# Second norm with a tile for each half's root, half 1 first, and the later fold instructions queued behind half 0's root

## The chip, the core and the metric

The kernel runs on one core of one Trainium2 chip. The metric is the device time of one execution in microseconds (us). TensorE (PE) multiplies matrices, VectorE (DVE), ScalarE (ACT) and GpSimd (POOL) work elementwise, and SyncE (SP) issues most of the loads; each engine takes its instructions in the order of its own queue, and a DMA issued from an engine's queue stands in that queue too.

## What is computed

The reference is a two-layer backbone over 1024 tokens of 1024 channels, in float32:

```python
for l in range(2):
    shift, scale, gate = split(silu(c) @ mod_w[l] + mod_b[l], 3)
    h = modulate(rmsnorm(x, norm_g[l]), shift, scale)        # h * (1 + scale) + shift
    if l == 0:  out = even_mixer(h, ...)   # convolution branch A and RG-LRU branch B, one out-projection
    else:       out = odd_mixer(h, ...)    # the pooling mixer, below
    x = x + gate * out
return rmsnorm(x, final_g)

def odd_mixer(h):
    u, g = split(h @ w_in, [2048])
    d = multiscale_pool(u)                 # four groups of 512 channels, each with its own window
    y = einsum("bngi,gij->bngj", d, w_grp) * scale
    return (y * silu(g)) @ w_out
```

`rmsnorm(x)` is x * rsqrt(mean over channels of x^2 + 1e-6) * g. The change is in the norm of the second layer, and in the tile of its helper, which the norm of the first layer uses as well.

## The kernel before

**Tiles.** x is held transposed: eight tiles of 128 channels by 1024 tokens, each in two halves of 512 tokens. Float32 products are made from rounded parts: `split` (line 101) writes the rounded high part with a cast on ScalarE (L102) and the rest with a subtract on the engine named (L103), and a product takes three matmuls, high-high, low-high and high-low. The out-projection `woa` and the v, g and wo products use `quad`, a seven-product scheme over 2 x 2 blocks whose weights `wquad` (lines 950 on) prepares from two loaded tiles `wr_...`, with sums such as `ws_v0` (L969).

**The folds.** The pooling mixer's group matrix and its input projection are both constant, so their product is formed once per group: `fold(g, ...)` (lines 236 to 263), a generator. It first loads the two halves of the group matrix (`graw_g_0`, `graw_g_1`), casts them on ScalarE (`gh`, L102) and subtracts on VectorE (`gl`, L103). That is the work up to its first `yield`. Then it loads four weight tiles (`wr_wu_g_0..3`) with the high part cast on ScalarE (`wh_wu`) and the low part on GpSimd (`wl_wu`), up to the second `yield`. Then for each of the four, and two strips of it, it runs 12 matmuls into a PSUM tile (`fold_g_kp_s`, L256 to L258), copies that on ScalarE (`fo_g_kp_s`, L261) and stores it to DRAM with a DMA from ScalarE's queue (L262), a `yield` behind every second strip. Groups 2 and 3 are left for this place. The stored products are the v weights that `wquad` loads later.

**Shared buffers.** `graw`, `wr_wu` and the `wr_v` tiles all use the pool tag "wr" with two buffers, so two chains of reuse run through the place: graw_3_0, wr_wu_3_0, wr_wu_3_2, wr_v0_0 in the one and graw_3_1, wr_wu_3_1, wr_wu_3_3, wr_v0_1 in the other. A load waits until the subtract that read the buffer's previous content is done, on VectorE for graw and on GpSimd for wr_wu. The `fo` tiles use a pool of two buffers: a copy waits for the store of the copy before the last.

**The norm.** Every out-projection row that is finished adds its square to `n1acc0` or `n1acc1` (L1265 on ScalarE, L1266 on VectorE), one for each half. `rstd_cols` (lines 194 to 208) then makes the root: four matmuls sum each column into one PSUM column (L200), ScalarE takes the Sqrt (L201, with a table load ahead of it), VectorE the reciprocal (L202) and a diagonal matrix `dg_...` (L204), and one matmul of ones with the diagonal puts the root into all 128 partitions (L207). The `rc` tile between Sqrt and diagonal has tag "rc" and one buffer in `hpool` and in `spool`, the same for both halves. After that, `scaled` (L1325) multiplies each tile half by the root and its channel scale on VectorE, 16 instructions in all; `split_x` (L1320 on ScalarE, L1321 and L103 on VectorE) makes the rounded parts of the block sums (`x_b11`, `x_t1`, `x_t3`, ...), and the quads for v (`qa_v`, `qb_v`, `qc_v`) multiply them with the folded weights. The tile `rc_n1h` and its like read `rc_n` in the profile, where the numbers at a name's end are left out (so also `dg_n`, `ms_n`, `gh`, `gl`).

**The order.** A scheduler places the instructions on each engine at build time, from the order of the program, from priorities, and from the context `tc.issue_after(ins)`: what is written inside comes behind `ins` in the queue, if it is on the engine of `ins`. In the program the column sums and roots of both halves (L1293) stand after the last out-projection product, and behind them come two steps of fold 2 and two of fold 3 (graw and weights), then the rest of both folds; the v stage follows. `load` (lines 106 to 114) puts every load on SP's queue.

**The first norm** (line 464) uses `rstd_cols` in the same way, with `rc_x`, `dg_x` and `ms_x`, at about 34 to 41 us of the span.

Of the kernel before, what the change touches and what calls it, by code (L numbers as in the profile page):

```python
# [9 lines left out]
F32 = mybir.dt.float32  # L10
F32R = mybir.dt.float32r
AF = mybir.ActivationFunctionType
# [3 lines left out]
P = 128  # L16
# [5 lines left out]
H = 512  # L22
# [33 lines left out]
def body(ctx, tc, xT, ctxT, cc, ccol, modT, modW, win, gw, wout, wu, grp, wg, wo1, small, edge, ident, outT):  # L56
    nc = tc.nc
    mult, add, sub = ALU.mult, ALU.add, ALU.subtract
# [22 lines left out]
    def ttile(name):  # L81
        return tpool.tile([P, H], F32, tag="t", name=name)

    def atile(name):
        return apool.tile([P, NR * PW], F32, tag="acc", name=name)

    def psum(name):
        return pm.tile([P, H], F32, tag="mm", name=name)
# [6 lines left out]
    def banks(name, n):  # L95
        if n % 2:
            t = wide(name)
            return [t[:, h] for h in HALF]
        return [pc.tile([P, H], F32, tag=f"c{i}", name=f"{name}_{i}") for i in range(2)]
# [46 lines left out]
    def col(o, n=1):  # L146
        return sm[:, o : o + n]
# [3 lines left out]
    eps_r = base.tile([P, 1], F32, name="eps_r")  # L151
# [39 lines left out]
        nc.vector.reciprocal(acc, rt[:, :n])  # L191


    def rstd_cols(acc, name, idD, rpool, wn):
        n = acc.shape[-1]
        nt = n // P
        ps, root = banks(f"ms_{name}", wn)
        r = rpool.tile([P, H // P], F32, tag="rc", name=f"rc_{name}")[:, :nt]
        for c in range(nt):
            nc.tensor.matmul(ps[:, c : c + 1], acc[:, c * P : (c + 1) * P], ones[:, 0:1], start=True, stop=True)  # L200
        nc.scalar.activation(r, ps[:, :nt], AF.Sqrt, bias=eps_r)  # L201
        nc.vector.reciprocal(r, r)  # L202
        t = ttile(f"dg_{name}")[:, :n]
        nc.vector.tensor_tensor(out=t.rearrange("p (c t) -> p c t", t=P),  # L204
                                in0=idD.unsqueeze(1).to_broadcast([P, nt, P]),
                                in1=r.unsqueeze(2).to_broadcast([P, nt, P]), op=mult)
        nc.tensor.matmul(root[:, :n], ones, t, start=True, stop=True)  # L207
        return root[:, :n]

# [25 lines left out]
    def fold(g, raw_tile, out_tile, g_tile=None, w_tile=None):  # L235
        g_tile = g_tile or dtile
        gh, gl = [], []
        for i in range(2):
            raw = raw_tile(f"graw_{g}_{i}")
            load(raw, grp[g, i])  # L240
            th = g_tile(f"gh_{g}_{i}", F32R)
            tl = g_tile(f"gl_{g}_{i}", F32R)
            split(raw, th, tl, nc.vector)
            gh += [th[:, 0:H], th[:, H:D]]
            gl += [tl[:, 0:H], tl[:, H:D]]
        yield
        if w_tile is not None:
            ws = [wload(wu[g, kp], f"wu_{g}_{kp}", nc.gpsimd, out=w_tile[kp]) for kp in range(KT // 2)]
            yield
        for kp in range(KT // 2):  # L250
            wh, wl = wload(wu[g, kp], f"wu_{g}_{kp}", nc.gpsimd) if w_tile is None else ws[kp]
            for s in range(2):
                ps = psum(f"fold_{g}_{kp}_{s}")
                for i in range(4):
                    kc = slice(i * 2 * P + s * P, i * 2 * P + (s + 1) * P)
                    nc.tensor.matmul(ps, wh[:, kc], gh[i], start=(i == 0), stop=False)  # L256
                    nc.tensor.matmul(ps, wh[:, kc], gl[i], start=False, stop=False)
                    nc.tensor.matmul(ps, wl[:, kc], gh[i], start=False, stop=(i == 3))  # L258
                dst = wfold[g][:, :, 2 * kp : 2 * kp + 2, :]
                o = out_tile(f"fo_{g}_{kp}_{s}")  # L260
                nc.scalar.copy(o, ps)  # L261
                nc.scalar.dma_start(dst[:, :, s, :].rearrange("m p c -> p m c"),  # L262
                                    o.rearrange("p (m c) -> p m c", c=P))
            yield
# [33 lines left out]
    with ExitStack() as sctx:  # L298
# [28 lines left out]
        acc = [atile("ssq0"), atile("ssq1")]  # L327
# [91 lines left out]
        for i, t in enumerate((cL, cC)):  # L419
            ps = banks(f"c_{i}", i)  # L420
# [41 lines left out]
        load(idx, ident)  # L462
        modulation(2)
        rx = [rstd_cols(acc[h][:, :H], f"x{h}", idx, spool, h) for h in range(2)]
        mod_row(1)
        mod_row(0)
# [186 lines left out]
    with ExitStack() as actx:  # L653
# [88 lines left out]
        for j in range(KT):  # L742
# [20 lines left out]
            name = "gb0" if final else f"xb{j + 1}"  # L763
# [6 lines left out]
            if state is None:  # L770
                for m in range(2 * KT, 3 * KT):
# [5 lines left out]
                    in1=col(O_MB + 2 * KT, KT), op=add)  # L777
# [9 lines left out]
            for h in range(2):  # L787
                ps = psum(f"va{j}_{h}")
# [5 lines left out]
            name = "gb1" if final else f"vg{j + 1}"  # L794
# [95 lines left out]
    hpool = ctx.enter_context(tc.tile_pool(name="hpool", bufs=1))  # L890
# [330 lines left out]
    for i in range(KH):  # L1221
        for j in (i, KH + i) if i else ():
# [3 lines left out]
            for h in range(2):  # L1226
                ps = psum(f"ga{j}_{h}")
# [30 lines left out]
    nacc = [atile("n1acc0"), atile("n1acc1")]  # L1258
# [24 lines left out]
    idD = cH[:, :P]  # L1283
# [3 lines left out]
    fold2 = fold(2, wr_tile, vtile, d2tile, [None, None, dtile, dtile])  # L1287
    fold3 = fold(3, wr_tile, vtile, d2tile, [dtile] * 4)
    for m in range(0, KT, 2):
        w0 = woa(m, w0, (lambda: wo_weights(m + 2)) if m < KT - 2 else None)  # L1290
    dsh = hpool.tile([P, KH], F32, name="dsh")
    nc.vector.tensor_tensor(out=dsh, in0=m1[:, 0, KH:KT], in1=m1[:, 0, 0:KH], op=sub)
    rs = [rstd_cols(nacc[h][:, :H], f"n1{h}", idD, hpool, h) for h in range(2)]  # L1293
    for f in (fold2, fold2, fold3, fold3):
        next(f)
    for f in (fold2, fold3):
        for _ in f:
            pass

    def ring_x(name):  # L1300
        return xpool.tile([P, S], F32R, tag="x", name=name)
# [37 lines left out]
    for i in range(KH):  # L1339
# [3 lines left out]
        t = block_sums(b11, b12, b21, b22, ttile(f"xt3_{i}"), nc.vector)  # L1343
# [343 lines left out]
    def last_half0(m, w, ahead=None):  # L1687
        p1, p2, p3, p4, p5, p6, p7 = w
        a, d, b = psum(f"qa_l{m}"), psum(f"qd_l{m}"), psum(f"qb_l{m}")
        (x0, x1_), (y0, y1) = [[x1[m + i][:, h] for h in HALF] for i in range(2)]  # L1690
        prod(a, p1, ops["b11"], True, False)
        with tc.high_priority(offset=EVAC):
            evac = nc.scalar.copy(b, a)
        mm = prod(d, p4, ops["t4"], True, True)
        with tc.high_priority(offset=EVAC):
            gated(m + 1, y0, d)
        nxt = None
        if ahead is not None:
# [20 lines left out]
    wb, _, _ = last_half0(m, wa, ahead)  # L1719
# [157 lines left out]
```

## Time and profile before

| what | value |
|---|---|
| time, median of 3 runs | 1294.53 us (1294.15 to 1294.73) |
| the profiled execution's own time | 1297.47 us |
| its span, first to last instruction | 1295.7 us |
| granted TensorE clock, mean | 0.996 |
| ScalarE, share of the span busy | 49% |
| GpSimd, share of the span busy | 27% |
| second norm's column sums of half 1 begin (PE) | 769.57 us |
| first Sqrt of the second norm (ACT) | 784.29 us |
| last fold matmul (PE) | 813.96 us |

The profile is of one execution. A row of a timeline names the start in us, the duration, the engine and source line, the operation, the tile written and those read, the shape, and in square brackets the idle time of the engine ahead of it with what ended that wait. `SPq` and `ACTq` are DMA issues from SP's and ScalarE's queues. `x16` at a row's end is a run of instructions of one kind, and the duration then is from the first to the last. A row of waits names what waited, for what, the sum, the number and the longest. Idle time of an engine matters only where PE waits for what that engine does.

### The profile page before, as it was taken

The page shows a single profiled execution, that of the slowest core. Times are in us where ns is not written, and L with a number is a line of the kernel's source. Part 1 is how long each engine was busy: PE and PEld are TensorE (multiplying, and loading weights), DVE is VectorE, ACT ScalarE, POOL GpSimd, SP SyncE. Part 2 cuts the span into 40 slices and gives each one's busy share as a digit, 9 for nine tenths or more (in the row PEclk, how much of TensorE's full clock was granted, in tenths as well). Part 3 has the DMA queues.
Part 4 walks back from the last instruction along what each step waited for, and adds up shares of the span by engine and source line. Part 5 has one row for each costly group of instructions (what it writes and reads, how often), then busy time and mean ns, then how long its engine had stood idle before and what let it go on. Part 6 is the DMA issues. An engine that isn't in the chain of part 4 may idle for free.

```text
span 1295.7 us, 15787 instructions
## 1 busy us (share of the span) xinstructions
PE 1274.6 (98%) x5630; PEld 1025.1 (79%) x5630; DVE 1143.5 (88%) x1758; ACT 637.3 (49%) x936; POOL 354.7 (27%) x180
## 2 busy tenths in 40 slices
PE   9999999999999999999999999999999999999997
PEld 4468888888888888888887887788888888778786
DVE  6979999999999989998789758998989987877876
ACT  4343666566657633237335346744334444644543
POOL 3063655575657613543210022000000000000002
PEclk9999999999999999999999999999999999999998
DMA  9934111121112133532555356244233324868723
GB/s 365 359 117 151 58 41 66 41 74 42 65 41 90 66 106 119 179 141 85 169 194 200 111 191 192 75 153 155 90 122 130 122 106 147 276 211 271 283 80 130
DMA packets 82899, 181.80 MB, mean 140 GB/s; under 512 B 7810, under 2 KB 27650, under 8 KB 82820
## 3 DMA queue, kind: packets, MB, share of 16 engines
q1 hardware_dynamic: 74372, 176.60, 39.4%
q10 hardware_dynamic: 8448, 4.20, 1.1%
q8 instruction: 44, 0.72, 0.2%
q14 instruction: 35, 0.29, 0.1%
HBM read 136.72 MB, written 44.04 MB: 140 GB/s over the span
## 4 chain that ended last, share of the span: by engine, by line
PE 76%; DMA 10%; DVE 8%; ACT 3%; issue 2%; POOL 1%; SPq 0%; POOLq 0%; DVEq 0%; ACTq 0%
PE vg L501 7%; PE wob L501 7%; PE va L501 7%; PE gb L501 7%; PE xb L501 6%; PE g L501 4%; PE fold L281 3%; PE ga L135 2%; PE ga L501 2%; PE ga L134 2%; PE ga L133 2%; PE xbc L501 2%; DMA x_part<-xp 1%; DMA wr_wo<-wo 1%; DMA mod<-modT 1%
## 5 line engine op out<-in xcount | busy, mean ns | idle before, releaser
L501 DVE SCALAR_TENSOR_TENSOR conv<-u,sm,conv 128x505 f32<-128x505 f32 (+6 forms) x224 | 153.7, 745 | 0.9
L1678 POOL TENSOR_TENSOR o<-x,rr 128x256 f32<-128x256 f32 (+1 forms) x10 | 9.6, 993 | 445.0 <-ACT rr L1614 445.0
L501 POOL TENSOR_TENSOR l<-l,l 128x1280 f32<-128x1280 f32 (+1 forms) x23 | 63.9, 2795 | 91.9 <-DVE l L501 76.8
L501 ACT ACTIVATE l<-g,sm 128x512 f32<-128x512 f32 (+1 forms) x96 | 58.5, 618 | 57.6 <-PE g L501 55.9
L281 PE MATMUL fold<-graw,wu 128*128 128x512 f32 x128 | 56.6, 603 | 0.0
L102 ACT CAST wq_g<-wr_g 128x512 fp32r<-128x512 f32 x48 | 28.2, 620 | 56.3 <-DVE wr_g L970 23.1
L501 PE MATMUL wob<-ybh,wh_wob 128*128 128x512 f32 x128 | 50.7, 396 | 0.0
L501 PE MATMUL gb<-h0h,wl_gb 128*128 128x512 f32 x128 | 49.9, 390 | 0.1
L501 PE MATMUL vg<-h0h,wl_vg 128*128 128x512 f32 x128 | 50.0, 391 | 0.0
L501 PE MATMUL gb<-h0h,wh_gb 128*128 128x512 f32 x128 | 49.9, 390 | 0.0
L501 PE MATMUL gb<-h0l,wh_gb 128*128 128x512 f32 x128 | 49.9, 390 | 0.0
L501 PE MATMUL wob<-ybh,wl_wob 128*128 128x512 f32 x128 | 49.9, 390 | 0.0
L501 PE MATMUL vg<-h0h,wh_vg 128*128 128x512 f32 x128 | 49.9, 390 | 0.0
L501 PE MATMUL vg<-h0l,wh_vg 128*128 128x512 f32 x128 | 49.8, 389 | 0.0
L501 PE MATMUL va<-h0h,wl_va 128*128 128x512 f32 x128 | 49.8, 389 | 0.0
L501 PE MATMUL va<-h0l,wh_va 128*128 128x512 f32 x128 | 49.8, 389 | 0.0
L501 PE MATMUL va<-h0h,wh_va 128*128 128x512 f32 x128 | 49.8, 389 | 0.0
L501 PE MATMUL wob<-ybl,wh_wob 128*128 128x512 f32 x128 | 49.8, 389 | 0.0
L501 DVE TENSOR_TENSOR_SCAN l<-l,l 128x256 f32<-128x256 f32 (+1 forms) x32 | 48.7, 1521 | 1.1
L103 POOL TENSOR_TENSOR wl_wu<-wr_wu,wh_wu 128x1024 fp32r<-128x1024 f32 x8 | 19.2, 2395 | 108.7 <-ACT wh_wu L102 108.1
L102 ACT CAST wq_v<-wr_v 128x512 fp32r<-128x512 f32 x48 | 28.2, 619 | 41.9 <-DMA wr_v<-wfold 16.5
L281 PEld LDWEIGHTS fold<-graw,wu 128*128 128x128 f32 x128 | 24.7, 195 | 29.9 <-issue 28.9
(611 smaller groups left out, 4361.0 us busy)
## 6 DMA issues: line engine op xcount, KB each, us to landing
mod<-modT SPq DMA_DIRECT2D x20, 512.0 KB, 5.8
x_part<-xp SPq DMA_DIRECT2D x32, 256.0 KB, 3.0
mod<-modT SPq DMA_DIRECT2D x32, 256.0 KB, 3.1
wr_v<-wfold SPq DMA_DIRECT2D x16, 512.0 KB, 3.6
wr_g<-wg SPq DMA_DIRECT2D x16, 512.0 KB, 4.3
wr_wo<-wo SPq DMA_DIRECT2D x16, 512.0 KB, 5.3
y_b<-y SPq DMA_DIRECT2D x24, 256.0 KB, 4.0
y_t<-y SPq DMA_DIRECT2D x24, 256.0 KB, 3.2
```

The costliest lines, as they stand in the source:

```text
L102: return (nc.scalar.copy(hi, src), eng.tensor_tensor(out=lo, in0=src, in1=hi.bitcast(F32), op=sub))
L103: eng.tensor_tensor(out=lo, in0=src, in1=hi.bitcast(F32), op=sub))
L133: nc.tensor.matmul(ps, hi[:, kc], xh[k][:, cols], start=(k == 0), stop=False)
L134: nc.tensor.matmul(ps, hi[:, kc], xl[k][:, cols], start=False, stop=False)
L135: nc.tensor.matmul(ps, lo[:, kc], xh[k][:, cols], start=False, stop=(k == ks - 1))
L281: nc.tensor.matmul(ps, w[:, kc], gs[i], start=(i == 0), stop=(i == 3))
L501: last[eng] = f(*args, **kw)
L1678: nc.gpsimd.tensor_tensor(out=outs[k // per][:, k % per], in0=x1[k][:, cols], in1=rr, op=mult)
```

## The change

`rstd_cols` gives each `rc` tile a tag of its own, so that the Sqrt of one half no longer needs the diagonal of the other to be done; this holds for both norms. It can also hand back the Sqrt and the diagonal instruction as marks. In the second norm half 1 is written ahead of half 0. Fold 2 makes three steps right behind it (its first pair of strips included); everything else of folds 2 and 3 is written inside `issue_after` of half 0's Sqrt and half 0's diagonal, so that on ScalarE the casts of fold 3 and the later copies and stores of fold 2 stand behind `rc_n10`, and on VectorE the subtracts `gl_3_0` and `gl_3_1` stand behind `dg_n10`. Fold 3's generator is now started ahead of fold 2's last three steps. What is computed is the same. Line numbers grow by 2 from L206 on, and by 9 behind the edit.

```diff
-    def rstd_cols(acc, name, idD, rpool, wn):
+    def rstd_cols(acc, name, idD, rpool, wn, marks=None):
...
-        r = rpool.tile([P, H // P], F32, tag="rc", name=f"rc_{name}")[:, :nt]
+        r = rpool.tile([P, H // P], F32, tag=f"rc_{name}", name=f"rc_{name}")[:, :nt]
...
-        nc.scalar.activation(r, ps[:, :nt], AF.Sqrt, bias=eps_r)
+        sq = nc.scalar.activation(r, ps[:, :nt], AF.Sqrt, bias=eps_r)
...
-        nc.vector.tensor_tensor(out=t.rearrange("p (c t) -> p c t", t=P),
+        dg = nc.vector.tensor_tensor(out=t.rearrange("p (c t) -> p c t", t=P),
...
+        if marks is not None:
+            marks += [sq, dg]
...
-    rs = [rstd_cols(nacc[h][:, :H], f"n1{h}", idD, hpool, h) for h in range(2)]
-    for f in (fold2, fold2, fold3, fold3):
-        next(f)
-    for f in (fold2, fold3):
-        for _ in f:
-            pass
+    marks, rs = [], {}
+    for h in (1, 0):
+        rs[h] = rstd_cols(nacc[h][:, :H], f"n1{h}", idD, hpool, h, marks)
+    for _ in range(3):
+        next(fold2)
+    with ExitStack() as rctx:
+        for mark in marks[2:]:
+            rctx.enter_context(tc.issue_after(mark.ins))
+        for f in (fold3, fold3, fold2, fold2, fold2):
+            next(f)
+        for f in (fold2, fold3):
+            for _ in f:
+                pass
```

The queues show what the scheduler made of it. On ScalarE, from the end of the out-projection on; `rc_n10` and `rc_n11` are the two Sqrts, `gh_3_i` and `wh_wu_3_i` the casts of fold 3 (the long number is the tile's own). Before:

```order
L261 COPY fo_2_0_1_6166<-fold_2_0_1_6153 128x512
L262 DMA wfold2_83<-fo_2_0_1_6166 128x4x128
L261 COPY fo_2_1_0_6182<-fold_2_1_0_6169 128x512
L102 CAST gh_3_1_6109<-graw_3_1_6107 128x1024
L262 DMA wfold2_83<-fo_2_1_0_6182 128x4x128
L261 COPY fo_2_1_1_6198<-fold_2_1_1_6185 128x512
L102 CAST wh_wu_3_0_6115<-wr_wu_3_0_6113 128x1024
L262 DMA wfold2_83<-fo_2_1_1_6198 128x4x128
L201 ACT_TABLE_LOAD
L201 ACTIVATE rc_n10_6044<-ms_n10_0_6042,eps_r_119 128x4
L201 ACTIVATE rc_n11_6055<-ms_n11_6054,eps_r_119 128x4
L102 CAST wh_wu_3_1_6121<-wr_wu_3_1_6119 128x1024
```

After, from the Sqrt of half 0 on (the table load and `rc_n11` now stand five and four rows ahead of it, behind the cast of wh_wu_2_3):

```order
L201 ACTIVATE rc_n10_6055<-ms_n10_0_6053,eps_r_119 128x4
L102 CAST gh_3_0_6135<-graw_3_0_6133 128x1024
L263 COPY fo_2_1_0_6182<-fold_2_1_0_6169 128x512
L263 COPY fo_2_1_1_6198<-fold_2_1_1_6185 128x512
L264 DMA wfold2_83<-fo_2_1_0_6182 128x4x128
L264 DMA wfold2_83<-fo_2_1_1_6198 128x4x128
L263 COPY fo_2_2_0_6214<-fold_2_2_0_6201 128x512
L264 DMA wfold2_83<-fo_2_2_0_6214 128x4x128
L102 CAST gh_3_1_6141<-graw_3_1_6139 128x1024
```

`gh_3_1` stood ahead of the Sqrts and now stands behind both, behind three copies of fold 2 and their stores. Further on, `wh_wu_3_0` follows fo_2_3_0, `wh_wu_3_1` follows fo_2_3_1, and `wh_wu_3_2` and `wh_wu_3_3` follow the first two copies of fold 3; the casts x_b11h of the v stage stand behind `wh_wu_3_3` in both orders.

On VectorE, around the two diagonals. Before, the subtracts of fold 3 stand ahead of both, and the scalings of half 0 and then of half 1 behind:

```order
L103 TENSOR_TENSOR gl_3_0_6104<-graw_3_0_6101,gh_3_0_6103 128x1024
L1266 TENSOR_TENSOR n1acc0_5486<-n1acc0_5486,n1q6_1_0_6037 128x512
L103 TENSOR_TENSOR gl_3_1_6110<-graw_3_1_6107,gh_3_1_6109 128x1024
L202 RECIPROCAL rc_n10_6044<-rc_n10_6044 128x4
L204 TENSOR_TENSOR dg_n10_6051<-cH_3640,rc_n10_6044 128x512
L202 RECIPROCAL rc_n11_6055<-rc_n11_6055 128x4
L204 TENSOR_TENSOR dg_n11_6062<-cH_3640,rc_n11_6055 128x512
L1325 SCALAR_TENSOR_TENSOR x1_0_5490<-x1_0_5490,a1_133,ms_n10_1_6043 128x512
```

After, from the sixth of the eight scalings of half 1 on; `dg_n11` stands ahead of all eight:

```order
L1334 SCALAR_TENSOR_TENSOR x1_6_5924<-x1_6_5924,a1_133,ms_n11_6042 128x512
L1334 SCALAR_TENSOR_TENSOR x1_3_5633<-x1_3_5633,a1_133,ms_n11_6042 128x512
L1334 SCALAR_TENSOR_TENSOR x1_7_5925<-x1_7_5925,a1_133,ms_n11_6042 128x512
L202 RECIPROCAL rc_n10_6055<-rc_n10_6055 128x4
L204 TENSOR_TENSOR dg_n10_6062<-cH_3640,rc_n10_6055 128x512
L103 TENSOR_TENSOR gl_3_0_6136<-graw_3_0_6133,gh_3_0_6135 128x1024
L103 TENSOR_TENSOR gl_3_1_6142<-graw_3_1_6139,gh_3_1_6141 128x1024
L1334 SCALAR_TENSOR_TENSOR x1_0_5490<-x1_0_5490,a1_133,ms_n10_1_6054 128x512
```

Both subtracts moved behind half 1's scalings and half 0's diagonal. Half 0's scalings are behind them, and what follows (x_b11l, wq_v, ws_v) is in the same order in both, up to the last x_t1l, which now stands behind the last x_t3l instead of ahead of it.

On PE, half 1's root now stands directly behind the last matmul of fold_2_1_1, one matmul of fold_2_2_0 ahead of half 0's column sums, and half 0's root is inside fold_2_3_1:

```order
L260 MATMUL fold_2_1_1_6185<-gh_2_1_6073,wl_wu_2_1_6086 128x512
L209 MATMUL ms_n11_6042<-dg_n11_6050,ones_117 128x512
L258 MATMUL fold_2_2_0_6201<-gh_2_0_6067,wh_wu_2_2_6091 128x512
L200 MATMUL ms_n10_0_6053<-ones_117,n1acc0_5486 128x1 x4
L259 MATMUL fold_2_2_0_6201<-gl_2_0_6068,wh_wu_2_2_6091 128x512
```

Before, half 0's sums stood behind the third matmul of fold_2_2_0, and both roots inside fold_2_3_0, four matmuls apart. SP issues the loads in the same order as before. In the first norm the second diagonal moves ahead of one small VectorE instruction (`a0`, L351); ScalarE's and PE's orders there are the same.

More of the change, by code (lines that the diff above doesn't have):

```diff
@@ L197, in rstd_cols @@
         ps, root = banks(f"ms_{name}", wn)
-        r = rpool.tile([P, H // P], F32, tag="rc", name=f"rc_{name}")[:, :nt]
+        r = rpool.tile([P, H // P], F32, tag=f"rc_{name}", name=f"rc_{name}")[:, :nt]
         for c in range(nt):
             nc.tensor.matmul(ps[:, c : c + 1], acc[:, c * P : (c + 1) * P], ones[:, 0:1], start=True, stop=True)
-        nc.scalar.activation(r, ps[:, :nt], AF.Sqrt, bias=eps_r)
+        sq = nc.scalar.activation(r, ps[:, :nt], AF.Sqrt, bias=eps_r)
         nc.vector.reciprocal(r, r)
         t = ttile(f"dg_{name}")[:, :n]
-        nc.vector.tensor_tensor(out=t.rearrange("p (c t) -> p c t", t=P),
-                                in0=idD.unsqueeze(1).to_broadcast([P, nt, P]),
-                                in1=r.unsqueeze(2).to_broadcast([P, nt, P]), op=mult)
+        dg = nc.vector.tensor_tensor(out=t.rearrange("p (c t) -> p c t", t=P),
+                                     in0=idD.unsqueeze(1).to_broadcast([P, nt, P]),
+                                     in1=r.unsqueeze(2).to_broadcast([P, nt, P]), op=mult)
+        if marks is not None:
+            marks += [sq, dg]
         nc.tensor.matmul(root[:, :n], ones, t, start=True, stop=True)
```

## The prediction

> **What bounds the kernel now.** I read the page first, for the engine that is busy throughout; then a table of windows over the stage that changes and the one after it; then PE's waits; then the timelines of the five engines from 769 to 826 us, to see what each waiting instruction waits for.
>
> ```profile
> PE 1274.6 (98%) x5630; PEld 1025.1 (79%) x5630; DVE 1143.5 (88%) x1758; ACT 637.3 (49%) x936; POOL 354.7 (27%) x180
> ...
> 780.00:790.00 10.00, 7.70 (x31) 5.39 (x30) 5.01 (x9) 6.40 (x9) 4.75 (x2) 1.00 0.57 187
> 790.00:815.00 25.00, 25.00 (x112) 20.70 (x111) 25.00 (x41) 16.96 (x30) 4.83 (x2) 1.00 0.55 166
> 815.00:840.00 25.00, 23.73 (x103) 18.80 (x102) 24.86 (x41) 19.06 (x32) 0.95 (x8) 1.00 0.21 74
> 840.00:1000.00 160.00, 159.46 (x704) 131.63 (x703) 148.58 (x270) 65.03 (x118) 0.00 (x0) 1.00 0.39 132
> ...
> PE ms_n L207 <- DVE dg_n L204: 2.3, 1, 2.3
> ```
>
> The columns of the window rows are the stretch, its length, then the busy time of PE, PEld, DVE, ACT and POOL, the granted clock (1.00 here), the DMA share and GB/s. PE is the bound, but from 790 to 840 us DVE has as little room: 25.00 of 25.00 us, then 24.86. Whatever starts this stretch late on DVE stays late to its end, and PE, 159.46 of 160 us busy afterwards, cannot make it up. The wait that the change aims at is the one of 2.3 us: PE's root matmul of half 0 waits for its diagonal.
>
> ```profile
> 773.38 1.05 ACT L102 CAST gh<-graw 128x1024 fp32r<-128x1024 f32 x1 [2.06 <-DMA graw<-grp]
> 774.86 0.57 ACT L261 COPY fo<-fold 128x512 f32<-128x512 f32 x1
> 777.28 1.05 ACT L102 CAST gh<-graw 128x1024 fp32r<-128x1024 f32 x1 [0.77 <-DMA graw<-grp]
> 784.29 0.26 ACT L201 ACTIVATE rc_n<-ms_n,eps_r 128x4 f32<-128x4 f32 x1
> 785.99 0.26 ACT L201 ACTIVATE rc_n<-ms_n,eps_r 128x4 f32<-128x4 f32 x1 [1.44 <-DVE dg_n L204]
> 786.15 1.03 ACT L102 CAST wh_wu<-wr_wu 128x1024 fp32r<-128x1024 f32 x1
> ...
> 778.36 1.23 DVE L103 TENSOR_TENSOR gl<-graw,gh 128x1024 fp32r<-128x1024 f32 x1 [2.07 <-ACT gh L102]
> 784.59 0.18 DVE L202 RECIPROCAL rc_n<-rc_n 128x4 f32<-128x4 f32 x1 [5.00 <-ACT rc_n L201]
> 784.80 1.16 DVE L204 TENSOR_TENSOR dg_n<-cH,rc_n 128x512 f32<-128x512 f32 x1
> 786.50 0.69 DVE L204 TENSOR_TENSOR dg_n<-cH,rc_n 128x512 f32<-128x512 f32 x1
> 787.18 10.62 DVE L1325 SCALAR_TENSOR_TENSOR x<-x,a,ms_n 128x512 f32<-128x512 f32 x16
> 800.98 0.68 DVE L969 TENSOR_TENSOR ws_v<-wr_v,wr_v 128x512 f32<-128x512 f32 x1
> ...
> 783.06 2.35 POOL L103 TENSOR_TENSOR wl_wu<-wr_wu,wh_wu 128x1024 fp32r<-128x1024 f32 x1 [9.26 <-ACT wh_wu L102]
> 787.27 2.40 POOL L103 TENSOR_TENSOR wl_wu<-wr_wu,wh_wu 128x1024 fp32r<-128x1024 f32 x1 [1.86 <-ACT wh_wu L102]
> 794.34 2.42 POOL L103 TENSOR_TENSOR wl_wu<-wr_wu,wh_wu 128x1024 fp32r<-128x1024 f32 x1 [1.92 <-ACT wh_wu L102]
> ...
> 779.61 0.33 SPq L112 DMA_DIRECT2D wr_wu<-wu  x1
> 796.78 0.33 SPq L955 DMA_DIRECT2D wr_v<-wfold  x1
> ```
>
> A second chain runs beside the roots. The last fold's weights and the first v weights share the two buffers of tag "wr", so they form two chains of load, split, load. The slower one is: graw_3_1 cast (gh, 777.28) and subtracted (gl, done at 778.36 + 1.23 = 779.59), so wr_wu_3_1 is loaded into that buffer (779.61), split (wl done at 787.27 + 2.40 = 789.67), then wr_wu_3_3 (wl done at 794.34 + 2.42 = 796.76), then wr_v0_1 (issued 796.78), which ws_v reads on DVE at 800.98. From there DVE has no gap worth the name to 840 us.
>
> **The change part by part.** *The roots.* Both Sqrts get a tile each, half 1 goes first, and the Sqrts leave the place behind the last fold casts. The removed 2.3 us of PE's wait and the 1.44 us of ACT's are real.
>
> ```profile
> 776.25 0.39 PE L256 MATMUL fold<-gh,wh_wu 128*128 128x512 f32 x1
> ...
> 776.93 0.95 PE L200 MATMUL ms_n<-ones,n1acc 128*128 128x1 f32 x8
> ...
> 786.01 1.13 PE L207 MATMUL ms_n<-dg_n,ones 128*128 128x512 f32 x2 [2.30 <-DVE dg_n L204]
> ```
>
> In the new order half 1's root stands ahead of fold_2_2_0, so at about 776.25 on PE. Its diagonal waits for nothing late: Sqrt behind one cast, done before 774, diagonal 0.69 to 1.16. The root takes 1.13, to 777.38; then one fold matmul (0.23, the step between the PE rows at 813.96 and 814.19 below), and half 0's column sums (0.95) end at 778.56.
>
> *What now stands behind them.* ACT: half 0's Sqrt (0.26) to 778.82, gh_3_0 (1.05) to 779.87, fo_2_1_0 (0.57) to 780.44, fo_2_1_1 (about the same) to 781.0, and only then the store of fo_2_1_0.
>
> ```profile
> DMA to landing us min/median/max: 2.3/2.4/5.1
> ...
> DMA to landing us min/median/max: 3.4/3.8/4.9
> ...
> DMA to landing us min/median/max: 3.2/3.6/5.0
> ```
>
> These three are the landings of the fold stores, of the wr_wu loads and of the wr_v loads. fo_2_2_0 needs the buffer of fo_2_1_0, so it waits to 781.0 + 2.4 = 783.4, and gh_3_1 is queued behind it: 783.4 + 0.57 + 0.37 for the issue + 1.05 = 785.4. On DVE the eight scalings of half 1 (16 take 10.62, so 5.3) run from 777.38 to 782.7, then half 0's reciprocal and diagonal (0.18 + 0.69) to 783.6, gl_3_0 (1.23) to 784.8, and gl_3_1 from 785.4 to 786.6. Before it ended at 779.59, so the buffer of graw_3_1 comes free 7.0 us later.
>
> Of that, 2.9 us come back, because before wr_wu_3_1 had landed by 779.61 + 3.8 = 783.4 and its cast lay behind the Sqrts to 786.15. Now wr_wu_3_0 is issued at 784.8, cast at 788.6 to 789.65, wl_3_0 on POOL (2.40) to 792.05. The cast of wh_wu_3_1 stands behind fo_2_3_1, which needs fold 2's end on PE: 778.56 + 47 x 0.23 + 1.13 for half 0's root = 790.5, copy to 791.1, cast to 792.1. So wl_3_1 ends at 792.1 + 2.40 = 794.5 (before 789.67, later by 4.8). wr_wu_3_3: 794.5 + 3.8 + 1.05 + 2.42 = 801.8 (before 796.76). wr_v0_1: 801.8 + 3.6 = 805.4, where ws_v starts: **4.4 us later** than 800.98. DVE's eight scalings of half 0 end long before that (786.6 + 5.3 = 791.9), and x_b11h stands on ACT behind the last wh_wu cast as before, so DVE idles some 8 us here instead of being early.
>
> *The end on PE.*
>
> ```profile
> 822.65 0.68 DVE L103 TENSOR_TENSOR x_t1l<-x,x_t1h 128x512 fp32r<-128x512 f32 x1
> 823.26 0.74 DVE L1321 SCALAR_TENSOR_TENSOR x_t3l<-xt,dsh,x_t3h 128x512 fp32r<-128x512 f32 x1
> ...
> 813.96 0.39 PE L258 MATMUL fold<-gh,wl_wu 128*128 128x512 f32 x1
> 814.19 0.39 PE L989 MATMUL qa_v<-x_b11h,wq_v 128*128 128x512 f32 x1
> ...
> 823.90 0.39 PE L991 MATMUL qc_v<-x_t1l,wq_v 128*128 128x512 f32 x1
> 825.19 0.50 PE L989 MATMUL qc_v<-x_b22h,wq_v 128*128 128x512 f32 x1 [0.67 <-ACT s_v L1033]
> ```
>
> The last x_t1l is done at 822.65 + 0.68 = 823.33 and PE uses it at 823.90: slack 0.57. The new order puts the last x_t3l ahead of it (823.92, where DVE went on, less 823.26: 0.66). So PE's use moves by 4.4 + 0.66 - 0.57 = +4.5. The 0.67 for s_v behind it stays, since s_v copies the product that this matmul ends. The removed 2.3 us of PE's wait lies ahead of this point and becomes waiting time there; so do waits in fold 3 for the late splits (each under 1 us by the times above). All these are priced at nothing, covered by DVE's lateness; if DVE were not late, the 2.3 would count.
>
> *First norm.*
>
> ```profile
> 37.25 0.69 DVE L204 TENSOR_TENSOR dg_x<-idx,rc_x 128x512 f32<-128x512 f32 x1
> 37.85 1.22 DVE L349 SCALAR_TENSOR_TENSOR junk<-mod,cC 128x1024 f32<-128x1024 f32 x1
> 39.00 0.17 DVE L202 RECIPROCAL rc_x<-rc_x 128x4 f32<-128x4 f32 x1
> 39.11 0.22 DVE L351 SCALAR_TENSOR_TENSOR a<-m,mb,sm 128x2 f32<-128x2 f32 x1
> 39.27 0.69 DVE L204 TENSOR_TENSOR dg_x<-idx,rc_x 128x512 f32<-128x512 f32 x1
> ```
>
> The second Sqrt no longer waits for dg_x0, but on DVE the 1.22 us product still stands ahead of dg_x1; only the small one at 39.11 moves behind it, 0.16 us. I take -0.15 (ends: 0, if the scalings behind the small one lose it again, and -0.16).
>
> *Sum.* 4.5 - 0.15 = +4.35. The profiled run took 1297.47 us (span 1295.7), 2.94 above the median; the sum is added to both: median 1294.53 + 4.35 = **1298.9**, span about 1300.0. With every landing at its least (3.4 and 3.2) ws_v is 3.6 late and the sum +3.5; with the ring's loads at their longest (4.9, 4.9, 5.0) wl_3_1 ends at 795.5, wl_3_3 at 803.9, ws_v starts at 808.9, and the sum is +7.9. I take the medians, since one load in place agrees: wr_wu_3_3, issued behind 789.67, had its split begun on POOL at 794.34, less a cast of 1.05: landed by 793.3, 3.6 later.
>
> One thing that DVE has no price for is x_b11l beside POOL: before, it began after POOL's last wl (796.76), now at about 800.4, inside POOL's wl_3_3 (to 801.8). The nearest row is the diagonal at 784.80, 1.16 us against 0.69, begun while POOL worked to 783.06 + 2.35 = 785.41: it ended about 0.55 after POOL did. If x_b11l waits like this, its four (0.66 each) run 801.8 to 804.4, wq_v to 805.1, and ws_v starts at 805.4 all the same or up to 0.4 later; I take nothing, +0.4 as the other end. The Trainium skill, "SBUF — State Buffer", section "Who interferes with whom", says that a VectorE instruction with two SBUF inputs and a GpSimd instruction that reads SBUF exclude each other, the later one blocked entirely; the row at 784.80 agrees. By that rule the sum would be some +4.5 instead of +4.35.
>
> **The rivals.** *A, faster.* Only the removed waits count: 2.3 + 0.15 gives 1292.1. For it speaks that ACT's wait behind the Sqrts (2.9 us in the wh_wu_3_1 cast) was itself in the ring. It needs the last x_t1l done by 823.90 - 2.3 = 821.6, so ws_v 2.4 us earlier than before, at 798.6; back through a load of 3.6, wr_wu_3_3's 7.27, wl_3_1's 2.40, a cast of 1.05 and a load of 3.8 that is gl_3_1 done by 780.5. Against it: eight scalings that need a root at 777.38 stand ahead of gl_3_1 and take 5.3 us. 6%.
>
> *B, no change.* The ring is late, but its loads land at their least (+3.5), and what PE idles behind x_t1l is used up by the new wait: the 0.67 for s_v at 825.19 and the 0.54 of 160 us after 840. +3.5 - 0.67 - 0.54 = +2.3, 1296.8. Also in here, at +0: that DVE's idle time is filled after all, the 2.3 us go, and a wait of that size takes their place in the folds. For it: the fold stores leave later, so the loads have less beside them. Against it: all landings must be at their least. 17%.
>
> *C, slower still.* The wr_wu loads of fold 3, now bunched with the fold stores, take 4.9 each, and DVE and POOL block each other: +7, 1301.5. It decides where a wr_wu lands over 4.4 us. 12%.
>
> *Forecast*, +2.7 to +6.5, about 65%: 1298.9, its own range 1297.4 to 1300.9.
>
> **How the numbers follow.** A measurement of this kernel tells about 0.2%, 2.6 us, from no change: 1291.9 to 1297.1. A (1292.1) lies just inside its lower edge, so faster gets 0.04 (A with a little more); the same gets the rest of A, B and the lowest part of the forecast, 0.19; slower 0.77. The range leaves out A and the upper half of C: 1294.6 to 1301.2.
>
> **What would show it.** Right: no wait of 2.3 us for dg_n; gl_3_1 ending near 786.6; POOL's last wl ending near 801.8; ws_v near 805.4 after some 8 us of idle DVE; new PE waits before 830 us, for x_t2l, x_b21l and x_t1l, that sum to 6 or 7 us; from 840 us on the same rows, some 4.5 later. Wrong: gl_3_1 before 781, or ws_v before 803, or PE reaching the last qc_v of x_t1l without waiting; then A or B holds. If wl_3_3 ends later than 803, C does.

## The result, and the profile after

The changed kernel takes 1300.97 us (median), the kernel before 1294.34 in the same comparison. The ratio is 1.0057, 95% interval 1.0039 to 1.0075: slower by 7.4 us, between 5.0 and 9.7. The medians differ by 6.6. One of the changed kernel's six executions took 4572.08 us and is not in the ratio; without it the median is 1300.77. The forecast was +4.35 us, with a range up to 1301.2 (+6.7): the sign and the mechanism held, the size was too small. The experiments below keep to the ratio.

The profiled execution of the changed kernel took 1299.57 us (span 1297.8), only 2.1 more than that of the kernel before. That pair understates the change, and two rows of each trace show where: the first product of the wo stage, over the columns count, shortest, median and longest duration, and first and last start. Before, then after:

```profile
L989 PE MATMUL qc_v<-x_b22h,wq_v x32: 388/389/502, 825.2 to 1096.7; 128*128 128x512 f32 x32
...
L989 PE MATMUL qa_wo<-y_b11h,wq_wo x24: 388/389/492, 1119.1 to 1216.6; 128*128 128x512 f32 x24
```

```profile
L991 PE MATMUL qc_v<-x_b22h,wq_v x32: 389/389/501, 831.7 to 1102.5; 128*128 128x512 f32 x32
...
L991 PE MATMUL qa_wo<-y_b11h,wq_wo x24: 389/389/389, 1124.9 to 1218.7; 128*128 128x512 f32 x24
```

The distance is 6.5 us at the first qc_v product with x_b22 and 5.8 us where the wo stage begins, but 2.1 us at its last qa_wo: the profiled execution of the kernel before lost 3.7 us inside the wo stage, in code that the change does not touch. That execution was 2.9 us above its kernel's median, as the prediction noted. In this pair what the change costs is therefore read at 825 to 1119 us. It is still only a pair: e6_first below, with the second norm's instructions in the order of the kernel before and a ratio of 0.9999, reaches the same qc_v product at 827.7, so a distance between two traces is good to some 2 us here, and the ratio decides.

The stage itself. First what DVE did in the changed kernel, from the scalings of half 1 to ws_v:

```profile
777.31 5.35 DVE L1334 SCALAR_TENSOR_TENSOR x<-x,a,ms_n 128x512 f32<-128x512 f32 x8 [2.26 <-PE ms_n L209]
...
782.79 0.70 DVE L204 TENSOR_TENSOR dg_n<-cH,rc_n 128x512 f32<-128x512 f32 x1
783.40 2.41 DVE L103 TENSOR_TENSOR gl<-graw,gh 128x1024 fp32r<-128x1024 f32 x2
789.31 5.36 DVE L1334 SCALAR_TENSOR_TENSOR x<-x,a,ms_n 128x512 f32<-128x512 f32 x8 [3.49 <-PE ms_n L209]
799.88 4.40 DVE L1330 SCALAR_TENSOR_TENSOR x_b11l<-x,m,x_b11h 128x512 fp32r<-128x512 f32 x4 [5.21 <-ACT x_b11h L1329]
804.20 0.68 DVE L103 TENSOR_TENSOR wq_v<-wr_v,wq_v 128x512 fp32r<-128x512 f32 x1
807.10 0.69 DVE L971 TENSOR_TENSOR ws_v<-wr_v,wr_v 128x512 f32<-128x512 f32 x1 [2.23 <-DMA wr_v<-wfold]
...
829.45 0.69 DVE L103 TENSOR_TENSOR x_t1l<-x,x_t1h 128x512 fp32r<-128x512 f32 x1
```

gl_3_1 ends at 783.40 + 2.41 = 785.8 (before 779.6). DVE then waits 3.5 us for half 0's root, 5.2 for x_b11h and 2.2 for the load of wr_v0_1, and ws_v begins at 807.10, 6.1 us later than before. Next, POOL's splits, SP's loads of the first v weights, and how long those two loads took to land (the changed kernel first, then the kernel before in the same part of its trace):

```profile
789.81 4.74 POOL L103 TENSOR_TENSOR wl_wu<-wr_wu,wh_wu 128x1024 fp32r<-128x1024 f32 x2 [15.91 <-ACT wh_wu L102]
796.97 4.77 POOL L103 TENSOR_TENSOR wl_wu<-wr_wu,wh_wu 128x1024 fp32r<-128x1024 f32 x2 [2.41 <-ACT wh_wu L102]
...
801.76 0.33 SPq L957 DMA_DIRECT2D wr_v<-wfold  x1
...
DMA to landing us min/median/max: 3.8/4.6/5.3
```

```profile
DMA to landing us min/median/max: 3.4/3.4/3.4
```

The last split ends at 796.97 + 4.77 = 801.74 and frees the buffer for wr_v0_1, issued at 801.76. It lands 5.3 us later, where before it took 3.4. Last, PE's waits and the stretch in which they fall (the columns of the windows as in the prediction):

```profile
PE qb_v L993 <- DVE x_t2l L1330: 1.6, 1, 1.6
...
PE qc_v L993 <- DVE x_t1l L103: 1.2, 2, 0.8
PE qa_v L991 <- ACT x_b21h L1329: 1.1, 1, 1.1
```

```profile
816.00:820.00 4.00, 2.75 (x9) 1.46 (x10) 4.00 (x8) 4.00 (x8) 0.01 (x1) 1.00 0.23 66
820.00:824.00 4.00, 1.25 (x5) 0.50 (x3) 4.00 (x7) 4.00 (x9) 0.00 (x0) 0.91 0.00 0
824.00:828.00 4.00, 4.00 (x10) 3.07 (x11) 4.00 (x7) 2.00 (x4) 0.00 (x0) 0.50 0.14 39
```

```profile
824.46 0.63 PE L994 MATMUL qb_v<-x_t2h,wq_v 128*128 128x512 f32 x1
824.88 0.63 PE L991 MATMUL qb_v<-x_t2h,wq_v 128*128 128x512 f32 x1
...
830.19 0.50 PE L993 MATMUL qc_v<-x_t1l,wq_v 128*128 128x512 f32 x1
```

The wait of 2.3 us for dg_n is gone from the list, and 3.9 us of new waits for the block sums stand in it. Then PE's granted clock (the figure ahead of the DMA share, 0.50 from 824 to 828 us) halves and the matmuls go from a step of 0.23 to one of 0.42. PE counts as busy there and is late all the same. The last x_t1l is done at 829.45 + 0.69 = 830.14 and PE uses it at 830.19, 6.3 us later than before (823.90).

### The profile page after: what moved, and what is told of

It is laid out like the page before. It is cut to its first block, busy times and chain, and to the rows that moved or that the text cites. A ratio compares the mean times of both kernels' runs of the same rounds, so it can differ in the third digit from the quotient of the medians.

```text
span 1297.8 us, 15781 instructions
## 1 busy us (share of the span) xinstructions
PE 1277.9 (98%) x5630; PEld 1026.7 (79%) x5630; DVE 1144.4 (88%) x1758; ACT 638.4 (49%) x936; POOL 354.0 (27%) x180
## 4 chain that ended last, share of the span: by engine, by line
PE 87%; DVE 6%; DMA 3%; ACT 2%; issue 1%; POOL 1%; POOLq 0%; ACTq 0%; DVEq 0%
PE gb L503 7%; PE vg L503 7%; PE wob L503 7%; PE va L503 7%; PE xb L503 6%; PE g L503 4%; PE fold L283 4%; PE ga L503 2%; PE qb_v L993 2%; PE qb_v L994 2%; PE qb_v L991 2%; PE xbc L503 2%; PE qb_g L993 1%; PE qb_g L994 1%; PE qb_g L991 1%
```

## The experiments

The theory to test is the forecast's: gl_3_1's place on DVE sets the chain of loads and splits through the two "wr" buffers (the ring, in the expectations), that sets ws_v, and from there DVE has no gap. Rivals: the casts and copies held on ScalarE; the order of the halves; the waits for the roots alone. Each kernel was compared with the kernel before; +x us below is the ratio of that comparison times the time before.

**e1_tile: the tiles alone.**

```diff
-        r = rpool.tile([P, H // P], F32, tag="rc", name=f"rc_{name}")[:, :nt]
+        r = rpool.tile([P, H // P], F32, tag=f"rc_{name}", name=f"rc_{name}")[:, :nt]
```

> The kernel before with one edit: each rc tile has its own tag; half 0 is still written first and nothing is held behind a root. The scheduler now puts the table load and half 1's Sqrt 10 us earlier and half 0's Sqrt directly ahead of the cast of wh_wu_3_1. Ring theory (the two buffers of tag wr, through gl and the low-part splits to ws_v, set the time): that cast no longer waits for a diagonal, so POOL's split of wh_wu_3_1 ends about 1.9 us earlier than 789.67, wr_v0_1 follows by as much, ws_v comes 1 to 1.9 us before 800.98, and the time falls by 0.8 to 2 us. Rival (the wait for the root on PE is what counts): the wait of 2.3 us shrinks to about 1, and the time falls by about as much, with ws_v where it was. Both see no loss: the loss of the whole change does not come from the tiles.

Ratio 1.0010 (0.9993 to 1.0027): no gain to be told, where both sides expected one. PE's waits for the diagonals, and DVE and POOL at that place:

```profile
PE ms_n L207 <- DVE dg_n L204: 3.6, 2, 2.2
...
783.01 5.33 DVE L204 TENSOR_TENSOR dg_n<-cH,rc_n 128x512 f32<-128x512 f32 x2
788.27 10.61 DVE L1325 SCALAR_TENSOR_TENSOR x<-x,a,ms_n 128x512 f32<-128x512 f32 x16
...
782.68 5.12 POOL L103 TENSOR_TENSOR wl_wu<-wr_wu,wh_wu 128x1024 fp32r<-128x1024 f32 x2 [9.21 <-ACT wh_wu L102]
```

The ring did come earlier: POOL's second split ended at 787.80, 1.9 us before the old 789.67, as forecast. But that put the two splits back to back, exactly where the two diagonals are made, and these took 5.33 us instead of 1.16 and 0.69. The scalings begin at 788.27 instead of 787.18, and ws_v at 802.06 instead of 800.98: DVE, not the load, set it.

**e3_graw and e10_gronly: fold 3's first step, and only it.** e3_graw takes the graw, gh and gl step out of the held part, e10_gronly leaves nothing but that step in it:

```diff
     for _ in range(3):
         next(fold2)
+    next(fold3)
     with ExitStack() as rctx:
...
-        for f in (fold3, fold3, fold2, fold2, fold2):
+        for f in (fold3, fold2, fold2, fold2):
```

```diff
             rctx.enter_context(tc.issue_after(mark.ins))
-        for f in (fold3, fold3, fold2, fold2, fold2):
-            next(f)
-        for f in (fold2, fold3):
-            for _ in f:
-                pass
+        next(fold3)
+    for f in (fold3, fold2, fold2, fold2):
+        next(f)
+    for f in (fold2, fold3):
+        for _ in f:
+            pass
```

> The changed kernel with one edit: fold 3's first step (graw loads, gh casts, gl subtracts) is written ahead of the context, so that it is not held behind half 0's root; weights, copies and stores of the folds stay held. Ring theory: gl_3_1 ends near 780 again, POOL's last split at or before 796.8, ws_v at or before 801, and the 6.6 us of loss are gone: the time is that of the kernel before or 1 to 2 us less, as the 2.3 us wait on PE stays removed. Rival 1 (the held casts and copies on ScalarE make the loss, with x_b11h behind them): the loss stays for the most part, +4 to +6. Rival 2 (half 1 first puts DVE's scalings in the wrong order): the loss stays too, +4 or more, since halves and scalings stay in the changed order.

> The changed kernel with the complement: only fold 3's first step (graw, gh, gl) is held behind half 0's root; weight casts, fold 2's copies and stores are written after the context and not held. Ring theory: gl_3_0 and gl_3_1 still stand on DVE behind half 1's scalings and half 0's diagonal, gl_3_1 ends after 785, and most of the loss stays: +4 to +7 us against the kernel before. Rival 1 (held casts and copies): the loss is mostly gone, +0 to +2. Rival 2 (order of halves): the loss stays, +4 or more; it is told from the ring by e3_graw.

e3_graw: ratio 0.9996 (0.9982 to 1.0010), the loss is gone. e10_gronly: 1.0040 (1.0025 to 1.0055), +5.2 us. The pair agrees with the ring theory and against the held casts and copies (held in e3_graw, not in e10_gronly) and the order of the halves (changed in both). In e3_graw, then e10_gronly, gl_3_1 or both subtracts, and ws_v:

```profile
777.25 1.22 DVE L103 TENSOR_TENSOR gl<-graw,gh 128x1024 fp32r<-128x1024 f32 x1 [0.68 <-ACT gh L102]
...
799.86 0.69 DVE L971 TENSOR_TENSOR ws_v<-wr_v,wr_v 128x512 f32<-128x512 f32 x1 [0.22 <-DMA wr_v<-wfold]
```

```profile
782.66 2.35 DVE L103 TENSOR_TENSOR gl<-graw,gh 128x1024 fp32r<-128x1024 f32 x2
...
806.74 0.69 DVE L971 TENSOR_TENSOR ws_v<-wr_v,wr_v 128x512 f32<-128x512 f32 x1 [1.88 <-DMA wr_v<-wfold]
```

gl_3_1 ends at 778.5 and at 785.0; ws_v starts 6.9 us apart. The hoped-for 1 to 2 us below the kernel before did not come in e3_graw: half 0's diagonal took 2.54 us there beside a split on POOL, x_t1l ended at 823.55, later than the old 823.33, and PE waits 2.7 us for it in place of the 2.3 for the diagonal.

**e9_nostore: the landing.** Four stores of fold 3 are left out (zeros are stored there earlier, so half of group 3's folded weights is zero). The second part of the edit, which stores the zeros, is not shown.

```diff
-                nc.scalar.dma_start(dst[:, :, s, :].rearrange("m p c -> p m c"),
-                                    o.rearrange("p (m c) -> p m c", c=P))
+                if (g, kp) not in ((3, 0), (3, 1)):
+                    nc.scalar.dma_start(dst[:, :, s, :].rearrange("m p c -> p m c"),
+                                        o.rearrange("p (m c) -> p m c", c=P))
```

> The changed kernel without the four stores of fold 3's first two weight tiles (zeros are stored in their place at about 700 us instead, so half of group 3's folded weights is zero). Ring theory with the landing as the missed term: wr_v0_1 was issued when forecast (801.76) but landed 5.3 us later where 3.6 was taken, beside two of these stores; without them it lands in 3.2 to 3.8 us, ws_v moves from 807.10 to about 805.3, and the time falls by 1.5 to 2 us against the changed kernel: +4.5 to +5.2 against the kernel before. Rival (the landing is not what ws_v waits for, or the 1.7 us are made up behind it): the time stays at +6 to +7.

The landing answered as expected, the time did not: 1.0068 (1.0046 to 1.0090), +8.8 us, more than either side gave. The landings of wr_v0_0 and wr_v0_1, ws_v, and PE's waits in the later g and v products:

```profile
DMA to landing us min/median/max: 3.2/3.2/3.2
...
805.88 0.69 DVE L972 TENSOR_TENSOR ws_v<-wr_v,wr_v 128x512 f32<-128x512 f32 x1
...
PE qb_g L992 <- ACT y L1499: 2.8, 2, 2.4
PE qb_v L992 <- ACT vp L1488: 2.0, 1, 2.0
...
L992 PE MATMUL qc_v<-x_b22h,wq_v x32: 389/389/497, 830.4 to 1105.8; 128*128 128x512 f32 x32
```

3.2 us instead of 3.8 and 5.3, no wait of ws_v for the load, and the product that began at 831.7 in the changed kernel begins at 830.4, though POOL's last split ended 0.9 later in this run (802.6). The two loads were issued 2.6 us apart here and 2.4 in the changed kernel, so their nearness alone isn't it: the stores beside them (issued at 800.96 and 803.32 there) belong to the late landing of wr_v0_1, as far as one trace of each shows. They are not enough either: in the kernel before three stores were issued around the same load (796.00, 798.23, 799.31), its loads 4.3 apart, and it landed in 3.4. Which meeting of loads and stores costs 1.9 us stays open. By the wo stage the kernel has lost 4.6 us against the changed one again (first qa_wo 1128.2 against 1124.9): with four DMAs less the scheduler placed later work on ScalarE and VectorE in another order, and PE waits for the ScalarE copies vp and y. So the shorter landing is shown, and the 1.3 us at 830 us are seen in one trace, within the scatter of traces, and not in the total.

**e6_first: the first norm alone.** `hpool_ref` holds the second norm's pool.

```diff
-        r = rpool.tile([P, H // P], F32, tag="rc", name=f"rc_{name}")[:, :nt]
+        r = rpool.tile([P, H // P], F32, tag=f"rc_{name}" if rpool is not hpool_ref[0] else "rc", name=f"rc_{name}")[:, :nt]
```

> The kernel before with the own tile in the first norm alone. Forecast of the sum: the second diagonal comes 0.16 us earlier on DVE, the time falls by 0 to 0.2 us, not to be told from no change. Rival: the earlier Sqrt lets the cast and copy behind it on ScalarE (modrow, h0h) start earlier, and the gain is up to 1 us.

0.9999 (0.9982 to 1.0016): nothing to be told. In the changed kernel's trace the second root matmul starts at 39.73 instead of 40.11, but part of these 0.4 us lies between the traces ahead of the edit. Counted from a VectorE product that stands ahead of the roots in all three (L349, L351 after; it begins at 33.50 before, at 33.34 in the changed kernel, at 33.99 here), the second root comes 6.61, 6.39 and 6.39 us later: the term is 0.2 us, near the 0.15 put in.

**e14_dgact and e15_e3dg: the diagonals on ScalarE,** on top of e1_tile and of e3_graw:

```diff
-        nc.vector.tensor_tensor(out=t.rearrange("p (c t) -> p c t", t=P),
-                                in0=idD.unsqueeze(1).to_broadcast([P, nt, P]),
-                                in1=r.unsqueeze(2).to_broadcast([P, nt, P]), op=mult)
+        for c in range(nt):
+            nc.scalar.activation(t[:, c * P : (c + 1) * P], idD, AF.Copy, scale=r[:, c : c + 1])
```

> e1_tile with the diagonals made on ScalarE (four scaled copies of the identity's 128 columns each, in both norms) instead of one VectorE product. In e1_tile the two diagonals began at 783.01 and took 5.33 us together, the first for as long as POOL's two splits ran (782.68 to 787.80), where they took 1.16 and 0.69 before. Lock theory (a two-input VectorE instruction and POOL exclude each other): without the VectorE diagonals PE's waits for dg_n shrink from 3.6 us to about 1 or less, ws_v comes some 2 us earlier than the 802.06 of e1_tile, and the time falls 1 to 3 us below e1_tile. Rival (the diagonals were late for the Sqrt's sake): the wait stays near 3 us.

> e3_graw with the diagonals made on ScalarE in the same way. In e3_graw half 0's diagonal took 2.54 us beside POOL's split, and half 0's scalings began at 790.64, DVE having idled 3.96 us for the root. Ring and lock theories: half 0's root stands earlier on PE, its scalings end before 795, ws_v starts when wr_v0_1 lands (near 799.8 or before), and the time is 0 to 3 us below the kernel before. Rival: the end of DVE's work is set by the loads of the v weights alone, and the time is that of e3_graw within 1 us.

e14_dgact: 1.0025 (1.0010 to 1.0039), +3.2 us; e15_e3dg: 1.0052 (1.0036 to 1.0068), +6.7 us. Both were forecast to gain and missed. In e14_dgact the lock theory was right about the waits: the one of 3.6 us for dg_n is gone, the scalings start at 785.25 instead of 788.27, and ws_v at 799.05, 3.0 earlier than in e1_tile. The product that starts at 825.2 in the kernel before starts at 823.5. All of it is lost by the wo stage (first qa_wo 1121.0, before 1119.1), again with a wait for vp:

```profile
PE qb_v L988 <- ACT vp L1471: 2.1, 1, 2.1
...
L988 PE MATMUL qc_v<-x_b22h,wq_v x32: 389/389/497, 823.5 to 1098.6; 128*128 128x512 f32 x32
...
L988 PE MATMUL qa_wo<-y_b11h,wq_wo x24: 389/389/389, 1121.0 to 1215.7; 128*128 128x512 f32 x24
```

In e15_e3dg the forecast failed at the stage itself: on ScalarE half 0's diagonal now stands ahead of the cast of wh_wu_3_0, POOL's first split of fold 3 starts at 786.26 where e3_graw's started at 780.28, the last ends at 800.4, and ws_v starts at 804.21.

**e2_half1: the halves' order alone,** with own tiles and nothing held:

```diff
-    rs = [rstd_cols(nacc[h][:, :H], f"n1{h}", idD, hpool, h) for h in range(2)]
+    rs = {h: rstd_cols(nacc[h][:, :H], f"n1{h}", idD, hpool, h) for h in (1, 0)}
```

> The kernel before with own tiles and half 1 written first; nothing is held behind a root, the folds are written as before. The scheduler leaves gl_3_1 ahead of half 1's scalings, as in e3_graw, but puts the first rounded v weight, wq_v0_1, ahead of half 0's eight scalings on DVE, and x_b11l behind ws_v. Theory (what starts late on DVE near 800 us stays late to 824): wq_v0_1 cannot start before its weights have landed and been cast, near 795 to 796, the eight scalings (5.3 us) come behind it, and DVE has 8 us of work left where the kernel before has 3.3 us: the last x_t1l ends near 826 and the time is +1 to +4. Rival (the ring alone): ws_v's load is issued at or before 796.8, so no loss, -2 to 0.

1.0030 (1.0015 to 1.0045), +3.9 us, at the upper end of what the theory gave, with a stage that is later than it gave: wq_v0_1 begins at 798.21, not near 796, and the last x_t1l ends at 829.75, not near 826. The ring is early here (wr_v0_1 issued at 796.2) and the kernel is slow all the same, since the scalings of half 0 stand behind wq_v0_1:

```profile
798.21 0.69 DVE L103 TENSOR_TENSOR wq_v<-wr_v,wq_v 128x512 fp32r<-128x512 f32 x1 [11.40 <-ACT wq_v L102]
798.81 5.35 DVE L1325 SCALAR_TENSOR_TENSOR x<-x,a,ms_n 128x512 f32<-128x512 f32 x8
```

So the ring is one way to make DVE late near 800 us; the lateness of DVE is what PE feels. In this trace PE is as late as in the changed kernel's (first qc_v product with x_b22 at 831.8 against 831.7, first qa_wo at 1125.2 against 1124.9); the two ratios' intervals overlap, so whether the two kernels differ at all is not shown.

**e11_both and e16_t1: is there a faster one?** e11_both also takes fold 3's weight casts out of the held part; e16_t1 adds another program order of the splits:

```diff
+    next(fold3)
+    next(fold3)
     with ExitStack() as rctx:
...
-        for f in (fold3, fold3, fold2, fold2, fold2):
+        for f in (fold2, fold2, fold2):
```

```diff
-        split_x("t3", i, t["t3"], dsh[:, i : i + 1], None)
         split_x("b22", i, b22, shift(KH + i), None)
-        split_x("t4", i, t["t4"], None, nc.vector)
+        later.append((t, i))
+    for t, i in later:
+        split_x("t3", i, t["t3"], dsh[:, i : i + 1], None)
+        split_x("t4", i, t["t4"], None, nc.vector)
```

> The changed kernel with fold 3's first two steps (graw, gh, gl and the weight loads with their casts) written ahead of the context; only copies and stores of the folds stay held behind half 0's root. Ring theory: in e3_graw the ring started early but the cast of wh_wu_3_2 waited 4.5 us behind a held copy, so POOL's splits stood still from 786.1 to 790.6; here the weight casts follow their loads more closely, wr_v0_1 is issued 1 to 3 us before 795.6, and the time falls to 1 to 3 us below the kernel before. Rival (from 801 us on DVE has 22 us of work in any order and PE waits for its end): the last x_t1l ends where it did, 823 to 824, since x_t1l now stands behind two x_t3l and two x_b21l, and the time is that of the kernel before within 1.5 us.

> e11_both with the program order of the block sums' splits changed: x_t3 and x_t4 are written in a second loop behind x_t1, x_t2 and x_b22. PE waits 2.4 us for x_t1l in e11_both. If those waits are DVE's order alone, the first of them (1.3 us) goes, since two of the four x_t3l now stand behind the second pair of x_t1l's first tile, and the time is 0 to 2 us below e11_both and -1 to -3 against the kernel before. If DVE's total work up to the last x_t1l sets it, the last x_t1l ends within 1 us of e11_both's (823.4), and the time is the same within 1 us.

e11_both: 0.9994 (0.9977 to 1.0011); e16_t1: 1.0008 (0.9993 to 1.0023). Neither is to be told from the kernel before. In e11_both the wait of 2.3 us for the diagonal is gone, PE finishes the folds 2.3 us earlier (last fold matmul 811.7), ws_v starts at 799.67, and the last x_t1l ends at 823.4 as before: PE waits 2.4 us for it. In e16_t1 that wait goes and another for x_t1h and qb_v comes. The rival that DVE's work up to the last x_t1l sets the time held both times (822.8 in e16_t1): with DVE full from 801 to 823 us, an earlier root has nothing to give PE.

## Why the prediction was wrong

- **What bounds the stage: right.** DVE had no gap from ws_v to the last x_t1l, the removed 2.3 us and fold 3's waits vanished into its lateness, and PE did not recover it (6.5 us at 825, 5.8 us at 1119).
- **The root of half 1, the held subtracts: right.** Scalings began at 777.31 (forecast 777.38); gl_3_1 ended at 785.8 (786.6). The store of fo_2_1_0 held gh_3_1 less than thought. Half 0's scalings were taken to follow gl_3_1 at once and began at 789.31 instead, behind a wait of 3.5 us for half 0's root; DVE had the time.
- **The ring to wr_v0_1's issue: right, to 0.1 us.** wl_3_1 ended at 794.55 (794.5), wl_3_3 at 801.74 (801.8), wr_v0_1 was issued at 801.76. Some of that is luck: wr_wu_3_1 was issued 0.8 us earlier than forecast and took 4.9 us to land instead of 3.8.
- **The landing of wr_v0_1: the step that failed.** "801.8 + 3.6 = 805.4, where ws_v starts" became 807.10. The term of 3.6 us, the median of its row, measured 5.3 in the profiled execution, above the row's longest (5.0), with a load 2.4 us ahead of it and two fold stores beside it; without the stores it took 3.2, and in e10_gronly, where loads and stores meet in the same way, 5.0. Rival C had bunched loads as its mechanism but named wr_wu: those landed in 3.6 to 4.9, the one of 4.9 held its cast up by 0.16 us, and C's sign, a wl_3_3 later than 803, did not show. The move of ws_v was forecast as 4.4 and measured 6.1.
- **The end on PE: right.** 6.1 + 0.66 - 0.57 = 6.2, measured 6.3 (830.19 against 823.90). The waits ahead of it were forecast to sum to 6 or 7 us and sum to 3.9: in the rest PE took 12 steps of 0.42 instead of 0.23 us, some 2.4 us that the prediction had as waiting. That the two last instructions changed places was read from the order, not tried by itself.
- **DVE beside POOL.** x_b11l's four took 4.40 us instead of 2.73, and the first took 2.41 us, to 802.29, 0.55 after POOL's split ended (801.74), as the row of 784.80 had suggested; DVE then waited 2.2 for the load, so it cost nothing here. The Trainium skill, "SBUF — State Buffer", section "Who interferes with whom", has the later of two such instructions blocked entirely; e1_tile agrees, where the diagonals took 2.58 and 2.83 us and each ended about 0.5 us after the split that it met.
- **First norm: about right.** 0.15 was put in, 0.2 is seen at its root matmul, below what e6_first can tell. By 770 us nothing of it is left between the two traces: the same cast of wh_wu begins at 770.27 before and at 770.38 after.
- **The sum.** With the landing measured the sum is +6.2, less at most the 0.2 of the first norm, inside the interval of the ratio (5.0 to 9.7). What stays open is whether the rest of 7.4 is anything but the width of that interval.

## What to carry to other kernels

Before moving work behind a root, follow every buffer that the moved work frees: here two subtracts of 1.2 us each stood at the head of a chain of load, split and load that ended 20 us later at the engine that had no gap. Removing a wait on the busiest engine gains nothing while the next engine's last operand comes when it came before. And where a change draws loads and stores together, do not cost the load that decides at the median of its row: here it took 5.3 us, and 5.0 in e10_gronly, against a median of 3.6 before. Last, check a distance between two traces against a third kernel that is the same at that place: e6_first came 2.5 us later out of a stage that its edit leaves as it was.

## What was not expected of the hardware

PE's clock. In six kernels in which PE waited near 820 us (the changed one, e9_nostore, e10_gronly, e15_e3dg, e2_half1 and e16_t1), its granted clock went to 0.50 soon after, and in the changed kernel the matmul step went from 0.23 to 0.42 us. In e10_gronly:

```profile
816.00:820.00 4.00, 3.11 (x10) 1.64 (x10) 4.00 (x7) 4.00 (x8) 0.00 (x0) 1.00 0.23 66
820.00:824.00 4.00, 1.13 (x4) 0.78 (x3) 4.00 (x8) 4.00 (x8) 0.00 (x0) 0.69 0.00 0
824.00:828.00 4.00, 4.00 (x11) 3.02 (x10) 4.00 (x8) 1.53 (x3) 0.00 (x0) 0.50 0.00 0
```

PE was busy 1.13 of 4 us and then ran at half its clock for 4 us and more. In the changed kernel this cost nothing, since x_t1l came no sooner (830.14); in e10_gronly x_t1l was done at 825.92 and PE, at half clock, used it at 827.56, so there the slow matmuls were part of the loss. In e3_graw the granted clock fell to 0.73 from 824 to 828 us. The kernel before, with 3.33 to 3.86 of 4 us busy in these windows, stayed at 1.00.

The wait alone does not decide it. e11_both was busy 2.68 and 2.95 of 4 us from 816 to 824 and stayed at 1.00. And the wait for the diagonal near 786 us, 2.3 us in the kernel before and 2.2 in e6_first, with the same order of instructions, was followed by full clock in the one and by slow steps in the other. The kernel before, then e6_first:

```profile
784.00:788.00 4.00, 1.99 (x7) 1.34 (x8) 3.01 (x6) 2.23 (x5) 2.14 (x2) 1.00 0.32 120
788.00:792.00 4.00, 4.00 (x18) 2.93 (x17) 4.00 (x7) 1.64 (x2) 3.65 (x2) 1.00 0.77 231
```

```profile
784.00:788.00 4.00, 1.78 (x6) 0.81 (x4) 2.16 (x4) 2.55 (x5) 2.26 (x1) 0.88 0.39 91
788.00:792.00 4.00, 4.00 (x11) 2.46 (x11) 3.20 (x6) 2.16 (x4) 3.36 (x2) 0.69 0.82 252
```

Of the 2.5 us by which e6_first is later at 827.7, 0.9 were there at the second norm's first column sums (770.5 against 769.6), and 1.6 came in this stage. So the wait that the change removes may cost more in other executions of the kernel before than in the profiled one; no run shows how often it does.

The Trainium skill, "TensorE: Matmul & The Clock Gate", section "🔬 Part 1: The HAM clock gate (the "warmup" mystery)", describes a gate that passes half the clock pulses when PE has not been busy; the granted clock of 0.50 and the longer step agree. No run here kept PE busy through the wait, so what the half clock costs by itself was not tried.

Second, VectorE and GpSimd: the two diagonals that took 1.16 and 0.69 us before took 5.33 us in e1_tile beside two splits that stood back to back, so that a change which starts POOL earlier can make DVE later.
